# A chunked RWKV-7 recurrence with its state and right-hand sides stored compactly: one head per partition half

## The chip, the cores and the metric

The kernel runs on one core of a Trainium2 chip. The metric is the device time of one execution in microseconds, the median of several runs. A second source is one profiled execution with a record of every instruction; its own time stands beside the median below. TensorE (PE) multiplies, VectorE (DVE), ScalarE (ACT) and GpSimd (POOL) do the elementwise work, SyncE (SP) issues most DMAs.

## The reference

One decoder layer for 256 tokens and a model width of 2048: a normalised input goes through one projection, whose columns feed an RWKV-7 mixer (16 heads of 64) and a latent attention (8 heads); both results are joined, projected and added; a gated feed-forward part with a short convolution follows. The change touches the RWKV-7 recurrence alone:

```python
def step(state, inp):
    r_t, w_t, k_t, v_t, a_t, b_t = inp
    sa = jnp.einsum('bhvk,bhk->bhv', state, a_t)
    state = (state * w_t[:, :, None, :]
             + sa[..., None] * b_t[:, :, None, :]
             + v_t[..., None] * k_t[:, :, None, :])
    return state, jnp.einsum('bhvk,bhk->bhv', state, r_t)

y = rwkv7_scan(r, decay, k, v, -kk, kk * a)
```

Here `kk` is a key divided by its norm, `kk * lax.rsqrt(jnp.maximum(jnp.sum(kk * kk), 1e-24))`. The state of a head is 64 by 64.

## The kernel before

Everything is fp32. Weights come in tiles of 128x1024; for each, SP loads `raw` (L132), ACT rounds it to `hi` (L138), DVE makes `lo = raw - hi` (L139), and PE multiplies `hi` and `lo` with activations (L168 to L202). This stream of weight tiles runs through the whole kernel: the 35 tiles of the input projection (`in_tile`), the tiles of the attention's up-projections (`up_b`), the output projection and the feed-forward part. The order of instructions on each engine is not written out by hand: a planner with a cost model of its own orders them, and each engine then runs its list strictly in order. So instructions of the recurrence stand between weight products on PE, and between casts on ACT and subtractions on DVE.

The recurrence is computed in four chunks of 64 tokens (`chunk(c)`), and in each chunk for two halves of the heads (`hf`), eight heads each. A half has four pairs `a_` of two heads `h`; head 0 of a pair lies on partitions 0 to 63, head 1 on 64 to 127. All products of a chunk come from line 700, with 64 output columns, head 0 to output partitions 0 to 63 and head 1 to 64 to 127, alternating between the heads.

- `px`, the right-hand side: the state times the keys (`state(0)`, from chunk 1 on), plus a local product of 128 rows (`local(0)`).
- `XB` (L711): the right-hand side, taken from `px` by DVE and multiplied there with `mtok`, the reciprocal squared key norms. XB has 128 rows and 128 columns for each pair, and the heads lie on its diagonal blocks; the other blocks were cleared once (L680). Two DVE instructions of 64 partitions each.
- `pu`: the inverse `TT` (128 rows) times XB. It is copied to `UV` by DVE for head 0 and by ACT for head 1 (L717).
- `pS`: the update of the state, 128 rows (keys and values of the chunk).
- `py`: the output, again a state product (`state(1)`) and a local one; ACT copies it to `yt` (L736).
- `ST`, the state: also block diagonal, 128 by 128 for each pair, cleared once (L675). DVE adds `pS` and multiplies with the decay `PC`, for each head by itself: four instructions of 64 partitions (L730, L731), two in chunk 0 (L733).

The inverse of a chunk's 64x64 unit triangular matrix is made ahead of the chunks. Its two 32x32 diagonal blocks are inverted by 31 steps of DVE (`solve`, L589 to L602); there the rows and columns of `Lp` are multiplied with `Mp`, the same norms in another layout (L596), and the diagonal of `Tq` starts at 1 (L594, POOL). The results go to `TT` and `T11` by DMA. The off-diagonal 32x32 corner then takes two sets of 64 small products. In the first (`pR`, L651) the heads alternate; DVE copies the result to `RT` and multiplies it with `mtok` (L655). The second (`pT`, L664) does 16 products of head 0, then 16 of head 1, and DVE copies it to `TT` (L668). Head 0 uses array rows 32 to 63 and columns 0 to 31 there, head 1 rows 96 to 127 and columns 64 to 95.

Behind the recurrence a group normalisation follows for each half of the tokens (L748), mostly on DVE, and then the output projection.

Of the kernel before, what the change touches and what calls it, by code (L numbers as in the profile page):

```python
# [9 lines left out]
F32 = mybir.dt.float32  # L10
# [4 lines left out]
ALU = mybir.AluOpType  # L15
AX = mybir.AxisListType

P = 128
# [36 lines left out]
def hybrid_layer(ctx: ExitStack, tc: tile.TileContext, a: dict, out: bass.AP):  # L55
    nc = tc.nc
    V, S, PE = nc.vector, nc.scalar, nc.tensor
    PSUM = bass.MemoryType.PSUM

    sb = ctx.enter_context(tc.tile_pool(name="sb", bufs=1))  # L60
# [5 lines left out]
    def nm(s):  # L66
        uid[0] += 1
        return f"{s}{uid[0]}"
# [3 lines left out]
    def s4(dt=F32, n="s4"):  # L72
        return sb.tile([P, 1024], dt, tag="s4", name=nm(n), bufs=NS4)

    def sv(n):
        return sb.tile([P, 1024], F32, tag="sv", name=nm(n), bufs=3)
# [13 lines left out]
    def t1(n, w=T, dt=F32):  # L90
        return sb.tile([P, 260], dt, tag="t1", name=nm(n), bufs=NT1)[:, :w]
# [10 lines left out]
    def ch(n="ch"):  # L102
        return ps.tile([P, 512], F32, tag="ch", name=nm(n), bufs=NCH)
# [4 lines left out]
    def con(shape, n, dt=F32):  # L108
        return sb.tile(shape, dt, name=n, bufs=1)
# [299 lines left out]
    AR = [s4(n="AR").rearrange("p (g c s t) -> p g c s t", g=2, c=4, s=2) for _ in range(4)]  # L409
    BK = [s4(n="BK").rearrange("p (g c s t) -> p g c s t", g=2, c=4, s=2) for _ in range(4)]  # L410
    PC = con([P, 8, 4], "PC")
# [46 lines left out]
    for h in range(2):  # L458
        hs = slice(h * 64, h * 64 + 64)
# [29 lines left out]
    mtok = con([P, 32], "mtok")  # L489
    Mp = con([P, 32], "Mp")  # L490
# [89 lines left out]
    TT = con([P, 32, 64], "TT")  # L580
# [8 lines left out]
    def solve():  # L589
        Lp = Lps[0]  # L590
        Tq = sv("Tq").rearrange("p (s t) -> p s t", s=32)
        tm = t1("tm")
        nc.gpsimd.memset(Tq, 0.0)
        nc.gpsimd.memset(Tq.rearrange("p s t -> p (s t)")[:, 0:1024:33], 1.0)  # L594
        nc.gpsimd.memset(TT, 0.0)
        V.tensor_tensor(Lp, Lp, Mp.unsqueeze(1).broadcast_to([P, 32, 32]), ALU.mult)  # L596
        for i in range(31):
            n, m = i + 1, 31 - i
            tv = tm[:, 0:n * m].rearrange("p (s t) -> p s t", s=n)
            V.tensor_tensor(tv, Tq[:, 0:n, i:i + 1].broadcast_to([P, n, m]),  # L600
                            Lp[:, i:i + 1, i + 1:32].broadcast_to([P, n, m]), ALU.mult)
            V.tensor_tensor(Tq[:, 0:n, i + 1:32], Tq[:, 0:n, i + 1:32], tv, ALU.add)  # L602
        dT = dr.tile([P, 32, 32], F32, name="dT")
        nc.sync.dma_start(dT, Tq)
        tp = sv("tp").rearrange("p (s t) -> p s t", s=32)
        V.tensor_copy(tp, Tq.rearrange("p s t -> p t s"))
        dU = dr.tile([2, 32, 32, 32], F32, name="dU")
        for h in range(2):
            T11.append(sv("T11").rearrange("p (q s) -> p q s", q=32))
        for h in range(2):  # L610
            nc.sync.dma_start(dU[h], tp[h * 64:h * 64 + 32])
        for h in range(2):
            nc.sync.dma_start(T11[h][64:96], dU[h].rearrange("q s t -> s q t"))
        for h in range(2):
            for b in range(2):
                k0 = h * 64 + b * 32
                nc.sync.dma_start(TT[k0:k0 + 32, :, b * 32:(b + 1) * 32], dT[k0:k0 + 32].rearrange("q s t -> s q t"))

    pend.append((0, solve_load))
    pend.append((1, solve))  # L620


# [21 lines left out]
    RT = sv("RT").rearrange("p (q s) -> p q s", q=32)  # L644
    for qh in range(2):
        pr_ = ch("pR")
        for q in range(16):
            qq = qh * 16 + q
            for h in range(2):
                o0 = h * 64 + 32  # L650
                PE.matmul(pr_[o0:o0 + 32, q * 32:(q + 1) * 32], G1[qq // 8][qq % 8 // 4][64:96, h * 4 + qq % 4, 32:64],  # L651
                          T11[h][64:96, qq, :], start=True, stop=True, tile_position=(64, o0))
        for h in range(2):
            o0 = h * 64 + 32
            V.tensor_tensor(RT[o0:o0 + 32, qh * 16:(qh + 1) * 16, :],  # L655
                            pr_[o0:o0 + 32].rearrange("p (q s) -> p q s", q=16),
                            mtok[o0:o0 + 32, qh * 16:(qh + 1) * 16].unsqueeze(2).broadcast_to([32, 16, 32]), ALU.mult)
    for qh in range(2):
        pr_ = ch("pT")
        for h in range(2):  # L660
            r0, o0 = h * 64 + 32, h * 64
            for q in range(16):
                qq = qh * 16 + q
                PE.matmul(pr_[o0:o0 + 32, q * 32:(q + 1) * 32], RT[r0:r0 + 32, qq, :],  # L664
                          TT[r0:r0 + 32, qq, 32:64], start=True, stop=True, tile_position=(r0, o0))
        for h in range(2):
            o0 = h * 64
            V.tensor_copy(TT[o0:o0 + 32, qh * 16:(qh + 1) * 16, 32:64],  # L668
                          pr_[o0:o0 + 32].rearrange("p (q s) -> p q s", q=16))


    yt = [sv("yt") for _ in range(2)]
    ST = [con([P, 4, P], f"ST{hf}") for hf in range(2)]
    for hf in range(2):
        nc.gpsimd.memset(ST[hf], 0.0)  # L675


    XB = [sb.tile([P, 512], F32, tag="xs", name=nm("XB"), bufs=2).rearrange("p (a t) -> p a t", a=4) for _ in range(2)]
    for hf in range(2):
        nc.gpsimd.memset(XB[hf], 0.0)  # L680
    HS = (slice(0, 64), slice(64, 128))

    ylast = [None] * 4
# [3 lines left out]
    def chunk(c):  # L687
        w, r = c // 2, c % 2
        rs_ = HS[r]
        for hf in range(2):  # L690
            px = ch("px")
            py = ch("py")

            def pairs(dst, terms):
                for n, term in enumerate(terms):
                    for a_ in range(4):
                        p = hf * 4 + a_
                        for h in range(2):
                            lhsT, rhs = term(p, a_, h)
                            PE.matmul(dst[HS[h], a_ * 64:(a_ + 1) * 64], lhsT, rhs,  # L700
                                      start=n == 0 and a_ == 0, stop=True, skip_group_check=True)

            def state(s):
                return lambda p, a_, h: (AR[p // 2][:, p % 2, c, s, :], ST[hf][:, a_, HS[h]])

            def local(s):
                return lambda p, a_, h: (G1[c][hf][:, h * 4 + a_, s * 64:s * 64 + 64], UV[c][:, p, HS[h]])

            pairs(px, ([state(0)] if c > 0 else []) + [local(0)])
            for h in range(2):  # L710
                V.tensor_tensor(XB[hf][HS[h], :, HS[h]], px[HS[h], 0:256].rearrange("p (a v) -> p a v", a=4),  # L711
                                mtok[HS[h], c * 8 + hf * 4:c * 8 + hf * 4 + 4].unsqueeze(2).broadcast_to([64, 4, 64]),
                                ALU.mult)
            pu = px[:, 256:512]
            pairs(pu, [lambda p, a_, h: (TT[:, c * 8 + p, :], XB[hf][:, a_, HS[h]])])
            for h in range(2):
                (S.copy if h else V.tensor_copy)(UV[c][64:128, hf * 4:hf * 4 + 4, HS[h]],  # L717
                                                 pu[HS[h]].rearrange("p (a v) -> p a v", a=4))
            if c < 3:
                pS = ch("pS")  # L720
                pairs(pS, [lambda p, a_, h: (BKt[c][:, p, HS[h]], UV[c][:, p, HS[h]])])
            pairs(py, ([state(1)] if c > 0 else []) + [local(1)])
            if c < 3:
                for h in range(2):
                    hs = HS[h]
                    sv = ST[hf][hs, :, hs]
                    pSv = pS[hs, 0:256].rearrange("p (a v) -> p a v", a=4)
                    pcb = PC[hs, hf * 4:hf * 4 + 4, c:c + 1].broadcast_to([64, 4, 64])
                    if c > 0:
                        V.tensor_tensor(sv, pSv, sv, ALU.add)  # L730
                        V.tensor_tensor(sv, sv, pcb, ALU.mult)  # L731
                    else:
                        V.tensor_tensor(sv, pSv, pcb, ALU.mult)  # L733
            for h in range(2):
                yv = yt[w][rs_, hf * 512:(hf + 1) * 512].rearrange("p (a h v) -> p a h v", a=4, h=2)
                ylast[c] = S.copy(yv[:, :, h, :], py[HS[h], 0:256].rearrange("p (a v) -> p a v", a=4)).ins  # L736
# [44 lines left out]
    for c in range(4):  # L781
        chunk(c)
# [199 lines left out]
    for blk, nf in enumerate((24, 20)):  # L982
        hh = [s4(F32R, "hh").rearrange("p (k t) -> p k t", k=4) for _ in range(nf // 4)]
        hl = [s4(F32R, "hl").rearrange("p (k t) -> p k t", k=4) for _ in range(nf // 4)]
        for fi in range(nf):
            f = f0 + fi
# [28 lines left out]
        for c in range(4):  # L1015
            accs = [mm() for _ in range(2)]
            for i in range(n - (4 if blk == 1 and c == 3 else 0)):
                prod_a(accs, piece(a["wdn"][c, f0 // 2 + i]), h_hi, h_lo, i * 2, 2, i == 0, i == n - 1)
                if blk == 1 and i == 2:
                    q = n - 4 + c  # L1020
# [98 lines left out]
```

## Time and profile before

| | us |
|---|---|
| median of 3 runs | 1200.92 (1199.66 to 1203.73) |
| profiled execution | 1200.7 |
| its span, first to last instruction | 1198.9 |

The page of the profile gives the busy time of each engine; PE's busy time is that of its matmuls and PEld's that of the loads of the stationary operand, which overlap them. The view by stage gives the same for chosen stretches of the span, with the granted TensorE clock (1.00 is full speed) and the share of the DMA engines. The chain that ended last lists, in order of time, the work that set the end: each piece is what released the next. The groups give, for each line and shape, the number of instructions, their busy time and mean, the idle time of the engine just before them, and what ended it. An fp32 matmul appears as two records.

In this profile the corner products run from about 233 to 244 us, and the four chunks from 244 to 316 us.

### The profile page before, as it was taken

Reading aid. Unit: us, or ns where it says so; the run is one execution under the profiler, and the core shown is the slowest. Engines: PE = TensorE matmul, PEld = TensorE weight load, DVE = VectorE, ACT = ScalarE, POOL = GpSimd, SP = SyncE. Lnnn points to the kernel's source line nnn. Section 1 sums busy time; section 2 is a strip of 40 time slices with the busy share of each in tenths; the row PEclk is TensorE's granted clock in tenths of the full one; section 3 lists DMA queues with packets and bytes.
Section 4 is the critical chain, followed back from the end, with each engine's and each line's share of the span. In section 5 each row is a group of like instructions: output and inputs, shape, how many; then the busy total and the mean of one; then the engine's idle time right before and its main releaser. Section 6 shows DMA issues by size and latency. Waiting matters only on the chain.

```text
span 1198.9 us, 19411 instructions
## 1 busy us (share of the span) xinstructions
PE 1168.8 (97%) x7673; PEld 1028.4 (86%) x7673; DVE 822.0 (69%) x1326; ACT 586.7 (49%) x887; POOL 33.2 (3%) x92
## 2 busy tenths in 40 slices
PE   9999999997989999999999999999999999999996
PEld 8899999996877888888888888888888888888885
DVE  5988669866986566777777775444577777775653
ACT  6694345432434455655555554333455555554541
POOL 1200000101000001000000000000000000000000
PEclk9999999989999999999999999999999999999999
DMA  9635455724333555655555565565655555566662
GB/s 315 217 106 177 133 171 191 229 90 128 107 106 123 178 179 171 206 187 191 192 190 194 189 197 180 193 196 188 209 188 188 191 191 191 194 226 204 209 210 82
DMA packets 71036, 215.99 MB, mean 180 GB/s; under 512 B 17616, under 2 KB 17872, under 8 KB 70944
## 3 DMA queue, kind: packets, MB, share of 16 engines
q1 hardware_dynamic: 69776, 211.84, 54.4%
q10 hardware_dynamic: 768, 2.05, 0.5%
q8 instruction: 60, 0.98, 0.4%
q0 software_dynamic: 400, 0.85, 0.3%
q14 instruction: 32, 0.26, 0.1%
HBM read 210.58 MB, written 3.41 MB: 178 GB/s over the span
## 4 chain that ended last, share of the span: by engine, by line
PE 91%; DVE 4%; DMA 2%; ACT 1%; POOL 1%; issue 1%; SPq 0%; ACTq 0%; DVEq 0%; POOLq 0%
PE mm L168 27%; PE mm L171 14%; PE mm L178 11%; PE mm L200 9%; PE mm L201 9%; PE mm L202 9%; PE mm L181 5%; DMA raw<-in_win 2%; PE pg L545 1%; DMA xt<-in_x 1%; DVE lo L139 1%; PE px L700 1%; ACT hi L138 0%; PE pT L664 0%; PE py L700 0%
## 5 line engine op out<-in xcount | busy, mean ns | idle before, releaser
L139 DVE TENSOR_TENSOR lo<-raw,hi 128x1024 fp32r<-128x1024 f32 x376 | 460.0, 1224 | 285.8 <-ACT hi L138 280.0
L138 ACT CAST hi<-raw 128x1024 fp32r<-128x1024 f32 x376 | 395.1, 1051 | 477.7 <-issue 146.8
L168 PE MATMUL mm<-z,hi 128*128 128x512 f32 x1408 | 351.2, 392 | 0.0
L168 PEld LDWEIGHTS mm<-z,hi 128*128 128x128 f32 x1408 | 251.9, 188 | 43.7
L171 PEld LDWEIGHTS mm<-z,lo 128*128 128x128 f32 x1408 | 188.2, 188 | 14.5
L171 PE MATMUL mm<-z,lo 128*128 128x256 f32 x1408 | 191.5, 278 | 0.0
L178 PE MATMUL mm<-x,hi 128*128 128x256 f32 x1024 | 138.8, 285 | 1.9 <-ACT hi L138 1.9
L178 PEld LDWEIGHTS mm<-x,hi 128*128 128x128 f32 x1024 | 126.8, 191 | 5.4 <-ACT hi L138 2.3
L201 PE MATMUL mm<-lo,hh 128*128 128x512 f32 x336 | 130.7, 389 | 0.0
L202 PE MATMUL mm<-hi,hl 128*128 128x512 f32 x336 | 130.7, 389 | 0.0
L200 PE MATMUL mm<-hi,hh 128*128 128x512 f32 x336 | 119.7, 389 | 0.0
L202 PEld LDWEIGHTS mm<-hi,hl 128*128 128x128 f32 x336 | 63.1, 188 | 13.2
L200 PEld LDWEIGHTS mm<-hi,hh 128*128 128x128 f32 x336 | 63.1, 188 | 13.0
L201 PEld LDWEIGHTS mm<-lo,hh 128*128 128x128 f32 x336 | 63.0, 188 | 13.0
L181 PE MATMUL mm<-x,lo 128*128 128x256 f32 x512 | 74.1, 283 | 0.0
L181 PEld LDWEIGHTS mm<-x,lo 128*128 128x128 f32 x512 | 65.7, 191 | 0.9 <-issue 0.7
L201 PE MATMUL mm<-lo,yhi 128*128 128x512 f32 x128 | 51.6, 403 | 0.0
L202 PE MATMUL mm<-hi,ylo 128*128 128x512 f32 x128 | 50.1, 393 | 0.0
L200 PE MATMUL mm<-hi,yhi 128*128 128x512 f32 x128 | 49.2, 402 | 0.0
L200 PEld LDWEIGHTS mm<-hi,yhi 128*128 128x128 f32 x128 | 23.9, 188 | 5.6 <-issue 0.8
L201 PEld LDWEIGHTS mm<-lo,yhi 128*128 128x128 f32 x128 | 24.1, 188 | 4.9 <-DVE lo L139 0.3
L202 PEld LDWEIGHTS mm<-hi,ylo 128*128 128x128 f32 x128 | 24.1, 188 | 4.9
(280 smaller groups left out, 1078.7 us busy)
## 6 DMA issues: line engine op xcount, KB each, us to landing
raw<-in_wgu SPq DMA_DIRECT2D x176, 512.0 KB, 3.4
raw<-in_wdn SPq DMA_DIRECT2D x88, 512.0 KB, 4.1
raw<-in_win SPq DMA_DIRECT2D x70, 512.0 KB, 3.8
raw<-in_wout SPq DMA_DIRECT2D x32, 512.0 KB, 3.5
raw<-in_wuq SPq DMA_DIRECT2D x6, 512.0 KB, 3.4
xraw<-in_xT SPq DMA_DIRECT2D x4, 512.0 KB, 6.8
xt<-in_x SPq DMA_DIRECT2D x4, 512.0 KB, 7.4
raw<-in_wuv SPq DMA_DIRECT2D x4, 512.0 KB, 3.3
```

Of the source, the lines that this page charges most:

```text
L138: S.copy(hi, raw)
L139: last_lo[0] = V.tensor_tensor(lo, raw, hi.bitcast(F32), ALU.subtract).ins
L168: PE.matmul(acc, hi[:, j * P:(j + 1) * P], act(kt0 + j), start=first and j == 0, stop=False, skip_group_check=True)
L171: PE.matmul(acc[:, :T], lo[:, j * P:(j + 1) * P], act(kt0 + j)[:, 0, :], start=False, stop=last and j == n - 1, skip_group_check=True)
L178: PE.matmul(acc[:, :T], hi[:, j * P:(j + 1) * P], act(kt0 + j)[:, s, :], start=first and j == 0 and s == 0, stop=False)
L181: PE.matmul(acc[:, :T], lo[:, j * P:(j + 1) * P], act(kt0 + j)[:, 0, :], start=False, stop=last and j == n - 1)
L200: PE.matmul(accs[tb], ah, wh, start=first and j == 0, stop=False)
L201: PE.matmul(accs[tb], ah, wl, start=False, stop=False)
L202: PE.matmul(accs[tb], al, wh, start=False, stop=last and j == n - 1)
L545: PE.matmul(pg[h][:, o:o + P], BK[pp][hs, gg, w * 2 + r, :, :], AR[pp][hs, gg, w * 2 + r, :, :], start=o == 0, stop=True, skip_group_check ...
L700: PE.matmul(dst[HS[h], a_ * 64:(a_ + 1) * 64], lhsT, rhs, start=n == 0 and a_ == 0, stop=True, skip_group_check=True)
```

## The change

State and right-hand side are no longer block diagonal. `ST` and `XB` hold 256 columns for a half: four pairs of 64, with head 0 on partitions 0 to 63 and head 1 on 64 to 127. The state products and the products with `TT` then take 64 rows for each head, instead of 128 rows of which half met zeros. The clearing of ST and XB is dropped. The updates of ST become one instruction for both heads.

The norms `mtok` are no longer multiplied onto XB and RT. The diagonal of `Tq` starts at `Mp` instead of 1, so that the inverse comes out with the norms in it. XB and RT are then plain copies: XB by DVE for half 0 and by ACT for half 1; RT and the corner of TT by DVE for head 0 and by ACT for head 1. In the second set of corner products the heads alternate.

```diff
-        nc.gpsimd.memset(Tq.rearrange("p s t -> p (s t)")[:, 0:1024:33], 1.0)
+        V.tensor_copy(Tq.rearrange("p s t -> p (s t)")[:, 0:1024:33], Mp)
...
-            V.tensor_tensor(RT[o0:o0 + 32, qh * 16:(qh + 1) * 16, :],
-                            pr_[o0:o0 + 32].rearrange("p (q s) -> p q s", q=16),
-                            mtok[o0:o0 + 32, qh * 16:(qh + 1) * 16].unsqueeze(2).broadcast_to([32, 16, 32]), ALU.mult)
+            (S.copy if h else V.tensor_copy)(RT[o0:o0 + 32, qh * 16:(qh + 1) * 16, :],
+                                             pr_[o0:o0 + 32].rearrange("p (q s) -> p q s", q=16))
...
-        for h in range(2):
-            r0, o0 = h * 64 + 32, h * 64
-            for q in range(16):
-                qq = qh * 16 + q
+        for q in range(16):
+            qq = qh * 16 + q
+            for h in range(2):
+                r0, o0 = h * 64 + 32, h * 64
                 PE.matmul(pr_[o0:o0 + 32, q * 32:(q + 1) * 32], RT[r0:r0 + 32, qq, :],
                           TT[r0:r0 + 32, qq, 32:64], start=True, stop=True, tile_position=(r0, o0))
         for h in range(2):
             o0 = h * 64
-            V.tensor_copy(TT[o0:o0 + 32, qh * 16:(qh + 1) * 16, 32:64],
-                          pr_[o0:o0 + 32].rearrange("p (q s) -> p q s", q=16))
+            (S.copy if h else V.tensor_copy)(TT[o0:o0 + 32, qh * 16:(qh + 1) * 16, 32:64],
+                                             pr_[o0:o0 + 32].rearrange("p (q s) -> p q s", q=16))
...
-    ST = [con([P, 4, P], f"ST{hf}") for hf in range(2)]
-    for hf in range(2):
-        nc.gpsimd.memset(ST[hf], 0.0)
+    ST = [con([P, 256], f"ST{hf}") for hf in range(2)]
...
-                return lambda p, a_, h: (AR[p // 2][:, p % 2, c, s, :], ST[hf][:, a_, HS[h]])
+                return lambda p, a_, h: (AR[p // 2][HS[h], p % 2, c, s, :], ST[hf][HS[h], a_ * 64:(a_ + 1) * 64])
...
-            for h in range(2):
-                V.tensor_tensor(XB[hf][HS[h], :, HS[h]], px[HS[h], 0:256].rearrange("p (a v) -> p a v", a=4),
-                                mtok[HS[h], c * 8 + hf * 4:c * 8 + hf * 4 + 4].unsqueeze(2).broadcast_to([64, 4, 64]),
-                                ALU.mult)
+            (S.copy if hf else V.tensor_copy)(XB[hf], px[:, 0:256])
             pu = px[:, 256:512]
-            pairs(pu, [lambda p, a_, h: (TT[:, c * 8 + p, :], XB[hf][:, a_, HS[h]])])
+            pairs(pu, [lambda p, a_, h: (TT[HS[h], c * 8 + p, :],
+                                         XB[hf][HS[h], a_ * 64:(a_ + 1) * 64])])
...
-                    if c > 0:
-                        V.tensor_tensor(sv, pSv, sv, ALU.add)
-                        V.tensor_tensor(sv, sv, pcb, ALU.mult)
-                    else:
-                        V.tensor_tensor(sv, pSv, pcb, ALU.mult)
+                if c > 0:
+                    V.tensor_tensor(ST[hf], pS[:, 0:256], ST[hf], ALU.add)
+                    V.tensor_tensor(s4v, s4v, pcb, ALU.mult)
+                else:
+                    V.tensor_tensor(s4v, pS[:, 0:256].rearrange("p (a v) -> p a v", a=4), pcb, ALU.mult)
```

Here `s4v` is ST of the half seen as four pairs of 64 columns.

More of the change, by code (lines that the diff above doesn't have):

```diff
@@ L667, in hybrid_layer @@
             o0 = h * 64
-            V.tensor_copy(TT[o0:o0 + 32, qh * 16:(qh + 1) * 16, 32:64],
-                          pr_[o0:o0 + 32].rearrange("p (q s) -> p q s", q=16))
+            (S.copy if h else V.tensor_copy)(TT[o0:o0 + 32, qh * 16:(qh + 1) * 16, 32:64],
+                                             pr_[o0:o0 + 32].rearrange("p (q s) -> p q s", q=16))
     yt = [sv("yt") for _ in range(2)]
-    ST = [con([P, 4, P], f"ST{hf}") for hf in range(2)]
-    for hf in range(2):
-        nc.gpsimd.memset(ST[hf], 0.0)
-    XB = [sb.tile([P, 512], F32, tag="xs", name=nm("XB"), bufs=2).rearrange("p (a t) -> p a t", a=4) for _ in range(2)]
-    for hf in range(2):
-        nc.gpsimd.memset(XB[hf], 0.0)
+    ST = [con([P, 256], f"ST{hf}") for hf in range(2)]
+    XB = [sb.tile([P, 512], F32, tag="xs", name=nm("XB"), bufs=2)[:, 0:256] for _ in range(2)]
     HS = (slice(0, 64), slice(64, 128))
@@ L723, in chunk @@
             if c < 3:
[L724 to L728, printed above, removed]
-                    if c > 0:
-                        V.tensor_tensor(sv, pSv, sv, ALU.add)
-                        V.tensor_tensor(sv, sv, pcb, ALU.mult)
-                    else:
-                        V.tensor_tensor(sv, pSv, pcb, ALU.mult)
+                pcb = PC[:, hf * 4:hf * 4 + 4, c:c + 1].broadcast_to([P, 4, 64])
+                s4v = ST[hf].rearrange("p (a v) -> p a v", a=4)
+                if c > 0:
[3 more added lines that the diff above has]
+                    V.tensor_tensor(s4v, pS[:, 0:256].rearrange("p (a v) -> p a v", a=4), pcb, ALU.mult)
             for h in range(2):
```

## The prediction

> **What bounds the kernel now.** I read the first two parts of the page, then the busy time by stage, then the chain that ended last inside the recurrence, and last the groups of instructions in that stretch.
>
> ```profile
> span 1198.9 us, 19411 instructions
> PE 1168.8 (97%) x7673; PEld 1028.4 (86%) x7673; DVE 822.0 (69%) x1326; ACT 586.7 (49%) x887; POOL 33.2 (3%) x92
> ```
>
> By the page PE is the bound: 97% of the span. That share is an average. The stages (columns: stretch, its length, busy time of PE, PEld, DVE, ACT, POOL, then the granted clock, the DMA share, GB/s) show where it is not true:
>
> ```profile
> 225.00:238.00 13.00, 13.00 (x220) 12.65 (x219) 8.12 (x13) 4.11 (x5) 4.49 (x14) 1.00 0.95 267
> 238.00:241.40 3.40, 2.79 (x82) 2.55 (x80) 2.92 (x6) 0.52 (x1) 0.00 (x0) 1.00 0.50 163
> 241.40:248.00 6.60, 6.56 (x80) 6.38 (x81) 2.67 (x5) 0.00 (x0) 0.00 (x0) 0.51 0.19 74
> 248.00:276.00 28.00, 28.00 (x306) 25.21 (x306) 18.28 (x32) 12.79 (x21) 1.77 (x5) 0.99 0.36 114
> 276.00:312.00 36.00, 25.79 (x520) 22.13 (x519) 27.25 (x59) 10.24 (x21) 3.94 (x14) 0.95 0.29 93
> 312.00:341.00 29.00, 29.00 (x217) 25.53 (x217) 22.66 (x39) 11.34 (x18) 0.00 (x0) 1.00 0.45 146
> 341.00:369.00 28.00, 22.90 (x97) 15.94 (x96) 20.81 (x53) 7.52 (x21) 0.00 (x0) 0.88 0.18 57
> 369.00:1199.00 830.00, 820.09 (x4329) 704.08 (x4327) 540.09 (x754) 408.28 (x596) 4.57 (x14) 1.00 0.58 189
> ```
>
> Three things stand out. After 369 us PE is full, and the change touches nothing there. At 241.4 to 248 PE is busy but at clock 0.51: about 3.2 of the 6.6 us are lost. At 276 to 312, where most of the recurrence runs, PE is idle for 10.2 of 36 us and DVE is busy for 27.25. So a microsecond counts in full before 276, where PE is the bound, and it counts in 276 to 312 if it lies on the chain of waits. What is gained there stays gained, since the weight products behind are in order on PE.
>
> The chain at the start of the recurrence (start, duration, work):
>
> ```profile
> 229.59 1.81 PE mm L178 x16
> ...
> 234.01 2.14 PE pR L651 x124
> ...
> 238.41 2.38 PE pT L664 x78
> 240.79 0.65 issue
> 241.44 2.60 PE pT L664 x50
> 244.04 1.05 PE px L700 x16
> 245.09 3.48 PE mm L178 x15
> ...
> 258.51 0.61 PE px L700 x16
> ...
> 292.03 0.47 PE py L700 x16
> ```
>
> and what DVE does in one round of it (a round is one half of the heads in one chunk; start, duration, instructions):
>
> ```profile
> 286.28 0.88 DVE L730 TENSOR_TENSOR ST<-pS,ST 64x256 f32<-64x256 f32 x2 [2.18 <-PE pS L700]
> 287.19 0.87 DVE L731 TENSOR_TENSOR ST<-ST,PC 64x256 f32<-64x256 f32 x2
> 288.09 0.69 DVE L757 TENSOR_REDUCE gmu<-yt 128x8 f32<-128x512 f32 x1
> 288.81 0.86 DVE L711 TENSOR_TENSOR XB<-px,mtok 64x256 f32<-64x256 f32 x2
> ```
>
> In this round the state takes four DVE instructions in a row and the row block XB two, and PE stands behind them. That is the serial part that the change shortens.
>
> **The change part by part.**
>
> *Corner products.* An fp32 product shows as two records. The pR products alternate between the heads' output columns and start every 2.14/124 = 17.3 ns. The pT products take all of one head, then the other, and start every 2.38/78 = 30.5 ns in the part before the clock falls. With the heads alternating I price all 128 at pR's spacing: 2.21 us. Now they take 2.38 + 2.60 = 4.98 us and a gap of 0.65 us, whose cause the profile doesn't show, so I leave it in. Saved 2.77. Then the clock: the pR run, of the same 32-row form and 2.14 us long, kept 1.00 (first row of stages); the fall comes after the longer pT run and its gap. With a run of 2.2 us I take it that the clock stays. Then px takes 0.61 and not 1.05 (saved 0.44), and 15 L178 products take 15/16 x 1.81 = 1.70 and not 3.48 (saved 1.78). Together 5.0 us, in a stretch where PE is the bound. Ends: 5.6 if the gap goes too; 1.9 if the clock falls as before (78 x 17.3 ns, 50 at twice that, and the gap make 3.7 against 5.6); 0 if alternating brings nothing, which is a rival.
>
> *XB and ST on 128 partitions.* The groups of 276 to 312 us:
>
> ```profile
> L711 DVE TENSOR_TENSOR XB<-px,mtok 64x256 f32<-64x256 f32 x10 | 4.2, 421 | 0.2
> L730 DVE TENSOR_TENSOR ST<-pS,ST 64x256 f32<-64x256 f32 x8 | 3.4, 420 | 3.7 <-PE pS L700 3.5
> L731 DVE TENSOR_TENSOR ST<-ST,PC 64x256 f32<-64x256 f32 x8 | 3.3, 418 | 0.2
> ...
> L190 DVE TENSOR_TENSOR qn<-mm,rrB 128x256 f32<-128x256 f32 x1 | 0.4, 425 | 0.0
> ```
> ```profile
> L717 ACT COPY UV<-px 64x256 f32<-64x256 f32 x4 | 1.5, 367 | 18.5 <-DVE UV L717 18.5
> ```
>
> An instruction of 256 columns takes 0.42 us on 64 partitions and on 128 (the L190 row), so two become one at the price of one. Of 10 XB instructions here, 4 belong to half 0 and become 2; 6 belong to half 1 and become 3 copies on ACT at 0.37 us. The 16 ST instructions become 8. DVE loses 8 x 0.421 + 4 x 0.420 + 4 x 0.418 = 6.7 us of its 27.25. On the chain one round gets shorter by half of each pair above: 0.44 + 0.43 + 0.43 = 1.3 us. There are four such rounds in the stretch (XB came ten times there, that is five pairs, and the last of them has no state behind it), so I take 4 x 1.3 = 5.2 us. The ends are 0, if something else holds the round (a rival), and the whole 6.7.
>
> What ACT takes over, and the wait ahead of the inverse (mean ns of one, then the idle time before):
>
> ```profile
> L138 ACT CAST hi<-raw 128x1024 fp32r<-128x1024 f32 x376 | 395.1, 1051 | 477.7 <-issue 146.8
> L655 DVE TENSOR_TENSOR RT<-pR,mtok 32x512 f32<-32x512 f32 x4 | 2.8, 690 | 1.4 <-PE pR L651 1.3
> L668 DVE COPY TT<-pT 32x512 f32<-32x512 f32 x4 | 2.7, 684 | 2.6 <-PE pT L664 2.6
> L596 DVE TENSOR_TENSOR Lp<-Lp,Mp 128x1024 f32<-128x1024 f32 x1 | 1.2, 1227 | 1.4 <-DMA Lp<-dL 1.4
> ```
>
> ACT gets four XB copies in the recurrence. It is busy 10.24 of 36 us in this stretch; what is queued behind a waiting copy there are the copies of U and y of the same half, which need its result anyway, and at times a weight cast, for which PE would wait. An XB copy stuck behind such a cast costs up to one cast, 1.05 us by the L138 row, times three.
>
> *RT and TT copies.* Two of each pair go from DVE to ACT, which runs them side by side. Cover: while RT is made (235.2 to 238.0), PE works on L178 and L181 products, so nothing is gained there; without that cover it would be 1.4 us (two instructions of 0.69 us, L655). TT's last copy ends before px's rows are needed.
>
> *Norms in the inverse.* The diagonal of Tq becomes one DVE copy of 32 elements instead of a GpSimd memset. It needs Mp and the cleared Tq, both long there, and DVE waits 1.4 us for Lp just before L596 (last row): cost nothing; uncovered, less than the 0.42 us of 256 columns. The dropped memsets of ST and XB were on an engine with 3% busy: nothing.
>
> *64-row products.* State and XB products, 192 + 128 = 320 records, go from 128 rows by 64 columns to 64 by 64. Heads already lie in different column halves, so two already run side by side; 16 records take 0.47 us (py at 292.03), 29 ns each. I take the same spacing after. Bounds: pR's 17.3 ns as a floor (320 x 12 ns = 3.8 us gain), and a loss that is the first rival.
>
> *Changes of row form on PE.* This is new. Now all products of a chunk have one form. After the change state products (64 rows) stand between local and pS products (128 rows). The weight loads show what a change of form costs:
>
> ```profile
> 232.91 0.20 PEld L651 LDWEIGHTS pR<-T,G 32*32 32x32 f32 x4
> 233.15 0.65 PEld L178 LDWEIGHTS mm<-x,hi 128*128 128x128 f32 x5
> 233.94 0.65 PEld L651 LDWEIGHTS pR<-T,G 32*32 32x32 f32 x36
> ```
>
> Four pR loads at 17 ns would let the next start at 232.98; it starts at 233.15. Five L178 loads at 1.81/16 = 113 ns would end at 233.72; pR starts at 233.94. So 0.2 us for each change, for 32x32 against the full array. [...]
>
> A round has four changes that no wait covers: pS to y-state and back, y-local to the next x-state, x-state to x-local. Two lie between the copy of U and the state update; the others run while DVE works on ST. So 2 x 0.2 x 4 rounds = 1.6 us on the chain, and 4 x 0.2 = 0.8 us for the round before 276, where PE is full: cost 2.4 us. Ends: 0, and all four changes in all six rounds with a state, 4.8.
>
> *Sum.* Profiled execution: 1200.7 us (span 1198.9 and 1.8 around it). 1200.7 - 5.0 - 5.2 + 2.4 = 1192.9. The median of the runs, 1200.92, lies 0.2 higher, so 1193.1.
>
> **The rivals.**
>
> *Slower: the two heads' 64-row products exclude each other.* Both heads write the same PSUM tile (px, py, one bank) from different row halves, as do the alternating pT products. In the kernel before, 64-row products of two heads (pg, L545) write two tiles. If two row halves can't write one bank at once, they run one after the other: the step from 17.3 to 30.5 ns between pR and pT is a factor 1.77, and 16 records go from 0.47 to 0.83 us. There are 12 state and 8 XB batches: 20 x 0.36 = 7.2 us, all taken as on the path. The corner products gain nothing and the clock falls as before. 1200.7 - 5.2 + 2.4 + 7.2 = 1205.1. The point from which it decides is (5.2 - 2.4)/20 = 0.14 us per batch. [...] Chance 0.13.
>
> *The round doesn't shrink.* DVE's freed time is refilled: gmu (at 288.09) already sits between ST and XB, and in 276 to 312 DVE has other normalisation work that goes into any gap; ACT's casts may hold XB. Then only the corner gains: 1200.7 - 5.0 + 2.4 = 1198.1. Chance 0.13.
>
> *The corner isn't freed.* Alternating gives no speed, or the clock falls all the same because the run of small products follows pR more closely: 1200.7 - 5.2 + 2.4 = 1197.9 at worst, 1196.0 with 1.9 kept. Chance 0.14.
>
> **How the numbers follow.** The forecast, 1193.1, has 0.60, and its own range is 1187 to 1197 (corner 5.6, DVE 6.7 and no cost of form give 1188.6, a third of the 3.8 for faster 64-row products 1187; 4.8 for form and a corner of 3.5, near the middle of its two ends with a gain, give 1197). The range reaches to the two rivals around 1198, and to 1201 for one of these with the dearer changes of form, and leaves out the slower one: 1187 to 1201. A measurement of this kernel can tell about 0.3%, 3.6 us, from no change; the borders are 1197.3 and 1204.5. Faster: 0.60 and half of the corner rival's 0.14, and a little of the other, 0.69. Slower: the first rival, 0.13; what part of it ends inside the border is made up by a tail in which the other two meet the dearer changes of form. The same: the rest, 0.18.
>
> **What would show it.** Right: the pT group in about 2.2 us with starts near 17 ns and a clock near 1.00 at 241 to 248; XB and ST as 128x256 instructions near 0.42 us, half as many; idle PE in the recurrence well under 10 us; gaps near 0.2 us where a state product follows a local one. Wrong: 64-row batches of 16 over 0.7 us; pT still at 30 ns; rounds between two copies of U as long as before with something new in the place of the second ST and XB; a new stop on ACT before XB; or a difference after 369 us, where this working expects none.

## The result and the profile after

| kernel | median, us | lowest to highest | runs |
|---|---|---|---|
| before | 1199.68 | 1196.34 to 1203.73 | 9 |
| after | 1193.76 | 1191.29 to 1195.77 | 9 |

The ratio after to before is 0.9949, 95% interval 0.9934 to 0.9963, a gain of 6.1 ± 1.7 us at 1200. The forecast was 1193.1 us. The profiled execution of the kernel after took 1195.8 us.

The page of the kernel after, its head and the busy time by engine:

```profile
span 1193.9 us, 19389 instructions
...
PE 1168.3 (98%) x7673; PEld 1027.1 (86%) x7673; DVE 809.4 (68%) x1301; ACT 590.0 (49%) x895; POOL 31.9 (3%) x87
```

PE has as many products as before. DVE has 25 instructions fewer. The span is 5.0 us shorter. Where it was saved is told by the first product of the feed-forward part (line 168). The view of that line shows the first and the last start, first in the kernel before:

```profile
L168 PE MATMUL mm<-z,hi x1408: 387/392/481, 462.8 to 1078.8; 128*128 128x512 f32 x176
```

and in the kernel after:

```profile
L168 PE MATMUL mm<-z,hi x1408: 387/392/481, 457.8 to 1073.8; 128*128 128x512 f32 x176
```

The first start is 5.0 us earlier and so is the last. All of the gain lies ahead of 458 us. It can be split at the corner. From the first pT record to the record behind the seventh L181 record that follows, both profiles do the same work on PE (128 records of pT, 16 of px, 15 of L178, 7 of L181). That took 10.87 us before and takes 9.95 after, which is 0.9 us. From there to the first L168 it was 213.6 us and is 209.3, which is 4.3 us. PE is busy for 198.3 and 198.5 us of that, so what shrank there is its idle time. (The pT products start 0.2 us later.) The stages of the kernel after, in the columns of the prediction:

```profile
238.00:241.40 3.40, 2.69 (x84) 2.29 (x82) 1.81 (x2) 1.08 (x2) 0.00 (x0) 1.00 0.59 233
241.40:248.00 6.60, 6.12 (x86) 5.94 (x87) 1.10 (x2) 1.85 (x3) 0.00 (x0) 0.55 0.25 83
...
276.00:312.00 36.00, 29.23 (x528) 24.66 (x524) 27.02 (x53) 13.09 (x27) 1.89 (x4) 1.00 0.33 105
...
341.00:369.00 28.00, 24.00 (x107) 17.20 (x106) 22.97 (x58) 9.98 (x28) 0.00 (x0) 0.94 0.24 78
```

In the recurrence (276 to 312) PE's idle time fell from 10.2 to 6.8 us. DVE's busy time there hardly moved (27.25 to 27.02): what it lost was filled with the next work of its list. The clock in this stretch is 1.00 and was 0.95, which the prediction did not count on. Against the forecast stands the second row: the clock is 0.55 behind the corner, where the prediction took 1.00. The chain that ended last shows the corner of this execution:

```profile
239.44 1.26 PE pT L663 x72
240.69 1.18 issue
241.88 1.62 PE pT L663 x54
243.50 1.05 PE px L695 x16
244.55 2.65 PE mm L178 x11
```

Each row is start, duration and work; "issue" is time in which PE waited for nothing that the profile shows. The pT products now start every 1.26/72 = 17.5 ns, as forecast. But the stop in their midst grew from 0.65 to 1.18 us, and the products behind it run at the lower clock: px takes 1.05 us, as before.

The rounds of the recurrence, from the same chain of the kernel after (px is the product with XB where it follows XB):

```profile
280.21 0.64 PE px L695 x16
...
284.93 0.33 DVE XB L705
...
290.52 0.38 ACT XB L705
...
292.19 1.23 DVE qr L829
293.42 1.15 DVE qs L830
294.59 1.22 DVE qr L831
295.81 0.35 DVE ST L720
296.18 0.43 DVE ST L721
...
298.22 0.34 DVE XB L705
```

and of the kernel before:

```profile
282.52 1.15 PE px L700 x16
...
289.24 0.44 DVE XB L711
...
295.22 0.44 DVE XB L711
...
302.54 0.43 DVE XB L711
```

XB was complete at 289.68, 295.66 and 302.97 before, and is at 285.26, 290.90 and 298.56 after. Taken from the first px, the rounds lasted 7.2, 6.0 and 7.3 us before and last 5.1, 5.6 and 7.7 us after. Two rounds shrank, by 2.1 and 0.4 us. Of the 2.1 us, most hangs on the point from which the round is counted: XB was ready 1.8 us ahead of that px after the change, while PE worked on other products, so from XB to XB this round shrank by 0.4 us only. The third grew by 0.4: three instructions of the attention's normalisation (qr, qs, qr) now stand ahead of ST there, where the chain before had the ST pair between qs and the second qr.

The groups of 276 to 312 us in the kernel after:

```profile
L721 DVE TENSOR_TENSOR ST<-ST,PC 128x256 f32<-128x256 f32 x4 | 1.7, 425 | 0.1
L720 DVE TENSOR_TENSOR ST<-pS,ST 128x256 f32<-128x256 f32 x4 | 1.7, 420 | 3.3 <-PE pS L695 3.3
L705 ACT COPY XB<-px 128x256 f32<-128x256 f32 x3 | 1.1, 373 | 1.0 <-PE px L695 1.0
L705 DVE COPY XB<-px 128x256 f32<-128x256 f32 x2 | 0.8, 416 | 0.0
```

An instruction of 256 columns on 128 partitions costs what one on 64 did (0.42 us on DVE, 0.37 on ACT). ACT begins these three XB copies when px is there; no weight cast held them.

### The profile page after: what moved, and what is told of

Its sections match the earlier page's. It is cut to its first block, busy times and chain, and to the rows that moved or that the text cites. A ratio compares the mean times of both kernels' runs of the same rounds, so it can differ in the third digit from the quotient of the medians.

```text
span 1193.9 us, 19389 instructions
## 1 busy us (share of the span) xinstructions
PE 1168.3 (98%) x7673; PEld 1027.1 (86%) x7673; DVE 809.4 (68%) x1301; ACT 590.0 (49%) x895; POOL 31.9 (3%) x87
## 4 chain that ended last, share of the span: by engine, by line
PE 92%; DVE 4%; DMA 2%; ACT 1%; issue 1%; POOL 0%; SPq 0%; ACTq 0%; DVEq 0%
PE mm L168 27%; PE mm L171 14%; PE mm L178 11%; PE mm L200 9%; PE mm L201 9%; PE mm L202 9%; PE mm L181 5%; PE pg L545 1%; PE px L695 1%; DMA xraw<-in_xT 1%; DMA xt<-in_x 1%; DVE lo L139 1%; PE py L695 1%; DMA raw<-in_win 0%; PE lw L426 0%
## 5 line engine op out<-in xcount | busy, mean ns | idle before, releaser
L168 PE MATMUL mm<-z,hi 128*128 128x512 f32 x1408 | 351.2, 392 | 0.0
L168 PEld LDWEIGHTS mm<-z,hi 128*128 128x128 f32 x1408 | 251.9, 188 | 43.7
L178 PE MATMUL mm<-x,hi 128*128 128x256 f32 x1024 | 139.0, 284 | 1.3 <-ACT x L148 1.2
L178 PEld LDWEIGHTS mm<-x,hi 128*128 128x128 f32 x1024 | 126.7, 191 | 5.0 <-issue 1.7
L181 PE MATMUL mm<-x,lo 128*128 128x256 f32 x512 | 75.1, 285 | 0.0
L181 PEld LDWEIGHTS mm<-x,lo 128*128 128x128 f32 x512 | 66.6, 193 | 1.0 <-issue 0.7
```

The source lines that it names most:

```text
L168: PE.matmul(acc, hi[:, j * P:(j + 1) * P], act(kt0 + j), start=first and j == 0, stop=False, skip_group_check=True)
L178: PE.matmul(acc[:, :T], hi[:, j * P:(j + 1) * P], act(kt0 + j)[:, s, :], start=first and j == 0 and s == 0, stop=False)
L181: PE.matmul(acc[:, :T], lo[:, j * P:(j + 1) * P], act(kt0 + j)[:, 0, :], start=False, stop=last and j == n - 1)
```

## The experiments

The prediction is the main theory; its view of the corner, half of the gain or more, is called B. Two rival theories stand beside it. A: all of the gain comes from the merged XB and ST (one instruction for both heads), and the corner is worth less than 1 us. C: the gain comes from 64-row products. The other letters are explained where they come up. Each ratio is to the kernel before, measured in the same group of runs. A difference of two ratios is given in us (times 1200), with the two half-widths added in squares. The planner orders the instructions of each kernel anew, so a difference between two kernels holds the new order as well.

| kernel | median, us (runs) | ratio, 95% interval |
|---|---|---|
| first group: before | 1199.32 (35) | |
| only the corner order changed (corner_alone) | 1197.56 (12) | 0.9982 [0.9967, 0.9997] |
| after, corner order as before (no_corner) | 1196.68 (12) | 0.9976 [0.9963, 0.9989] |
| after, XB and ST one instruction for each head (split_heads) | 1200.74 (12) | 1.0015 [0.9998, 1.0032] |
| the same with 128-row products (rows128) | 1198.10 (12) | 0.9989 [0.9975, 1.0003] |
| second group: before | 1199.84 (23) | |
| after again (after_again) | 1193.46 (8) | 0.9948 [0.9930, 0.9967] |
| after, more warm-up products (shift64) | 1204.07 (10) | 1.0043 [1.0023, 1.0062] |
| before with compact, merged XB and ST (merge_alone) | 1197.18 (12) | 0.9986 [0.9970, 1.0002] |
| after, py's local products first (order_py) | 1192.31 (6) | 0.9938 [0.9913, 0.9963] |
| third group: before | 1200.37 (14) | |
| after, py's local products first (order_again) | 1193.62 (9) | 0.9949 [0.9928, 0.9969] |
| after a third time (after_third) | 1194.19 (6) | 0.9949 [0.9930, 0.9968] |
| before, one execution (before_look) | 1198.10 (1) | |
| no_corner, one execution (no_corner_look) | 1195.94 (1) | |

**The corner alone, and everything but the corner.** The first kernel is the one before with the two loops of the pT products exchanged:

```diff
-        for h in range(2):
-            r0, o0 = h * 64 + 32, h * 64
-            for q in range(16):
-                qq = qh * 16 + q
+        for q in range(16):
+            qq = qh * 16 + q
+            for h in range(2):
+                r0, o0 = h * 64 + 32, h * 64
                 PE.matmul(pr_[o0:o0 + 32, q * 32:(q + 1) * 32], RT[r0:r0 + 32, qq, :],
```

The second is the kernel after with the opposite edit.

> The kernel before with one edit: the second set of corner products (pT) alternates between the heads. Theory A (the whole gain of the change comes from XB and ST being one instruction for both heads; the corner gives under 1 us, because PE stops inside the run for something that is not a product, and the clock falls in any case): pT records start every 17 ns instead of 30, the stop inside the run grows from 0.65 to about 1.2 us, the clock still falls to half for about 6.8 us, time within 1 us of before (1199.7). Theory B (the corner carries half or more of the gain): 1195 to 1197, with a shorter stretch at half clock.

> The changed kernel with the second set of corner products undone (16 of one head, then 16 of the other). Theory A: at most 1 us slower than the changed kernel, 1194 to 1195. Theory B: it loses half of the gain or more, 1196.5 to 1199.

Measured: the corner alone saves 2.2 ± 1.8 us (ratio 0.9982). Taken out of the kernel after, it costs 0.9976 - 0.9949 = 0.0027, that is 3.2 ± 2.4 us. A's bound of 1 us lies inside both intervals, and so does B's half (3 us), so the medians alone decide little: they put the corner at some 2 to 3 us, not 5. The profiles say more. The stretch of equal work described above took 9.8 to 10.9 us in the five profiles with the old order (mean 10.5). With the new order it took 6.2 to 6.9 us in the six profiles in which the clock stayed at 1.00 behind the corner (mean 6.5), and 9.3 to 10.0 us in the three in which it fell (mean 9.6). So the order is worth 4.0 us where the clock stays, 0.8 us where it falls, and 2.9 us on the average of the nine. That speaks against A and puts the corner near B's half. A had also expected the clock to fall in corner_alone, where it stayed at 1.00 (with a stop of 0.94 us). The chain of no_corner shows what the order costs when the clock falls:

```profile
236.93 2.38 PE pT L663 x78
239.31 0.27 issue
239.57 1.97 PE pT L663 x50
241.54 1.05 PE px L695 x16
242.60 3.50 PE mm L178 x15
```

These are the 30.5 ns of the kernel before (2.38/78), and the same 1.05 and 3.5 us behind them.

**The merged instructions and the row form.** The third kernel keeps everything of the kernel after but gives each head its own XB and ST instruction on 64 partitions (`HS[h]` and `hs` are the rows of a head):

```diff
-            (S.copy if hf else V.tensor_copy)(XB[hf], px[:, 0:256])
+            for h in range(2):
+                (S.copy if hf else V.tensor_copy)(XB[hf][HS[h]], px[HS[h], 0:256])
...
-                    V.tensor_tensor(ST[hf], pS[:, 0:256], ST[hf], ALU.add)
-                    V.tensor_tensor(s4v, s4v, pcb, ALU.mult)
+                        V.tensor_tensor(ST[hf][hs], pS[hs, 0:256], ST[hf][hs], ALU.add)
+                        V.tensor_tensor(s4v, s4v, pcb, ALU.mult)
```

The fourth makes ST and XB block diagonal again on top of that, so that all products of a chunk have 128 rows; the norms in the inverse, the ACT copies and the corner order are what is left of the change:

```diff
-                return lambda p, a_, h: (AR[p // 2][HS[h], p % 2, c, s, :], ST[hf][HS[h], a_ * 64:(a_ + 1) * 64])
+                return lambda p, a_, h: (AR[p // 2][:, p % 2, c, s, :], ST[hf][:, a_, HS[h]])
...
-            pairs(pu, [lambda p, a_, h: (TT[HS[h], c * 8 + p, :],
-                                         XB[hf][HS[h], a_ * 64:(a_ + 1) * 64])])
+            pairs(pu, [lambda p, a_, h: (TT[:, c * 8 + p, :], XB[hf][:, a_, HS[h]])])
```

> The changed kernel with XB and ST made by one instruction for each head again (64 partitions each, same engines, same 64-row products). Theory A: each of four rounds gets 1.3 us longer, PE idle in the recurrence goes back from 6.8 towards 10 us, 1198 to 1200. Theory C (the gain is that of the 64-row products on PE): 1194, no slower than the changed kernel.

> As split_heads, but state and XB block diagonal again, with 128-row products: only the norms in the inverse, plain copies and the corner are left of the change. Theory A: no changes of row form on PE, so it is 1 to 2.5 us faster than split_heads (0.16 us for each change of form, two to four in a round, six rounds), 1196 to 1198. Theory C: slower than split_heads, 1199 to 1201.

Measured: without merging the kernel is 1.0015 - 0.9949 = 0.0066 slower than the kernel after, 7.9 ± 2.7 us, and slower than the kernel before or equal to it. 64-row products in place of 128-row ones cost 1.0015 - 0.9989 = 0.0026, 3.1 ± 2.6 us; they save nothing, which speaks against C, as does the time without merging (C forecast 1194). What is left in rows128 beyond the corner (norms, ACT copies) is 0.9989 - 0.9982 = 0.0007, 0.8 ± 2.5 us, no difference that this can tell from nothing. So by these differences the merging is the whole net gain beside the corner, and the compact layout that makes it possible costs some of it.

How merging saves its time is only in part what the prediction says. The stage of the recurrence in split_heads:

```profile
276.00:312.00 36.00, 27.40 (x445) 23.70 (x445) 27.89 (x55) 12.81 (x26) 0.00 (x0) 0.89 0.22 70
```

The granted clock in this stretch is 0.86 to 0.95 in the five profiles with XB and ST by head (0.95 before and in corner_alone, 0.86, 0.91 and 0.89 in before_look, rows128 and split_heads). In the nine with merged instructions it is 1.00 six times and 0.95 three times. By the means, 0.91 and 0.98, that is up to 0.07 x 36 = 2.5 us, an estimate from above, since PE is idle in part of the stretch. What keeps the clock up there was not tested.

**The price of a change of row form.** The weight loads of PE in one round of the kernel after (start, duration; the form is in the middle):

```profile
288.50 0.55 PEld L695 LDWEIGHTS py<-UV,G 128*64 128x64 f32 x14
289.12 0.54 PEld L695 LDWEIGHTS px<-ST,AR 64*64 64x64 f32 x16
289.74 0.55 PEld L695 LDWEIGHTS px<-UV,G 128*64 128x64 f32 x16
```

and in the kernel before, where both have 128 rows:

```profile
277.74 0.60 PEld L700 LDWEIGHTS px<-ST,AR 128*64 128x64 f32 x16
278.21 0.60 PEld L700 LDWEIGHTS px<-UV,G 128*64 128x64 f32 x16
```

From the first state load to the first local load it is 0.62 us now and was 0.47: 0.15 us for the change, against 0.2 for the other pair of forms in the prediction. K is the theory that each change costs its 0.16 us in full, L that the changes are hidden in PE's idle time. An edit takes two of the four changes of a round away: the local products of py ahead of its state products, so that the next px state products follow their own form:

```diff
-            pairs(py, ([state(1)] if c > 0 else []) + [local(1)])
+            pairs(py, [local(1)] + ([state(1)] if c > 0 else []))
```

> The changed kernel with the two terms of py exchanged: local products first, then state products, so that on PE the state products of py and of the next px stand together and a round has two uncovered changes of row form instead of four. Theory K (a change of form costs 0.16 us of PE, on the chain or where PE is full): six rounds x 2 x 0.16 = 1.9 us less, 1191.5 to 1193. Theory L (they are hidden in PE's idle time, and state products as filler while U is copied are worth more): the same as the changed kernel or up to 2 us slower.

> The kernel after with the local products of py ahead of its state products, so that the next right-hand side's state products follow products of their own form: two changes of form fewer in each round. Theory K (a change of form costs 0.16 us where PE is the last to arrive: two fewer in four rounds on the chain and in the round before): 1.3 to 1.6 us less than the kernel after in the same call. Theory L (hidden behind DVE's state update): no difference, within 0.5 us. The first run of this edit stood 1.2 us below, with overlapping intervals.

In its loads the two changes are gone (order_again):

```profile
286.52 0.54 PEld L695 LDWEIGHTS py<-ST,AR 64*64 64x64 f32 x16
286.98 0.55 PEld L695 LDWEIGHTS px<-ST,AR 64*64 64x64 f32 x16
287.60 0.55 PEld L695 LDWEIGHTS px<-UV,G 128*64 128x64 f32 x16
```

State follows state after 0.46 us. In 276 to 312 us PE's idle time is 36.00 - 31.11 = 4.9 us, against 6.8 in the third execution of the kernel after. First order_again, then after_third:

```profile
276.00:312.00 36.00, 31.11 (x489) 27.39 (x488) 27.52 (x52) 13.81 (x26) 0.00 (x0) 1.00 0.37 117
```

```profile
276.00:312.00 36.00, 29.23 (x501) 24.87 (x502) 26.93 (x52) 13.26 (x28) 0.46 (x1) 1.00 0.32 103
```

These windows do not hold the same work, though: the last copy of y ends at 317.2 us in order_again and at 311.4 in after_third, so other weight products stand in between. By the medians the edit saves 1.2 us in the second group and 0.6 in the third; the intervals overlap in both, and in the third the two ratios are equal (0.9949). The loads show that the changes are gone; whether that saves time is not settled between L's 0 and K's 1.6 us.

**Everything but the norms, the ACT copies and the corner.** The kernel before with compact ST and XB, one DVE instruction for both heads, and the norms still multiplied onto XB:

```diff
-            for h in range(2):
-                V.tensor_tensor(XB[hf][HS[h], :, HS[h]], px[HS[h], 0:256].rearrange("p (a v) -> p a v", a=4),
-                                mtok[HS[h], c * 8 + hf * 4:c * 8 + hf * 4 + 4].unsqueeze(2).broadcast_to([64, 4, 64]),
-                                ALU.mult)
+            V.tensor_tensor(XB[hf].rearrange("p (a v) -> p a v", a=4), px[:, 0:256].rearrange("p (a v) -> p a v", a=4),
+                            mtok[:, c * 8 + hf * 4:c * 8 + hf * 4 + 4].unsqueeze(2).broadcast_to([P, 4, 64]), ALU.mult)
```

and ST and its products as in the kernel after. J is the theory that XB's move to ACT counts, too.

> The kernel before with compact ST and XB only: 64-row products, one instruction for both heads, XB always by VectorE and still multiplied with the norms there; the norms in the inverse, the copies on ScalarE and the alternating corner are left out. Theory A (the merged instructions carry the gain, the norms and ScalarE nothing): as fast as the changed kernel without the corner, 1195.5 to 1197.5. Theory J (taking XB of half 1 off VectorE counts too): 1198 to 1199.5.

Measured: 1.7 ± 1.9 us faster by the ratio, 2.7 by the medians. The prediction's terms for this edit are -5.2 + 2.4 = -2.8 us. That is not told apart from no change by itself, but agrees in size, and the median of 1197.18 lies where A expected it (1195.5 to 1197.5), not J (1198 to 1199.5). By the ratios J is not settled: what this kernel lacks against the kernel after (corner, norms, ACT copies) is 0.9986 - 0.9949 = 0.0037, 4.4 ± 2.6 us, of which the corner's 2 to 3 us leave about 2, inside the error.

**The stop and the clock in the corner.** The kernel after was run twice more. The expectations weigh two theories on the fall of the clock: F, it belongs to the order of the products, against G, it is chance. (So the letters stand from after_third on; in after_again G stands for the kernel's order.) They also weigh H, PE's stop is a block of its instructions that comes late, against I, it belongs to the products.

> The changed kernel once more, beside the next ones. All theories: 1193 to 1195. [...] Theory G (the fall belongs to this kernel's order): the same fall as in the first profile.

> The kernel after once more, as the comparison for the new order and as a third look at the corner. Theory F (the fall of the clock behind the corner belongs to the head-by-head order and to a long stop): 1.00 in the stretch behind the corner. Theory G (it is chance in either order): 1.00 or 0.5, as in the first two looks.

> The kernel before, one look, for the clock behind the corner. Theory F: it falls to about 0.5 again for some 7 us, as in the three profiles with the head-by-head order so far. Theory G: 1.00 in about half of the looks; then the medians hold only half of the 2.2 us that the first profile shows behind the corner.

> The kernel after with the second set of corner products head by head again, a second look, for the clock. Theory F: falls to about 0.5. Theory G: 1.00 in about half of the looks.

The corner of after_again, from the chain and from the stages:

```profile
240.29 1.26 PE pT L663 x72
241.55 0.36 issue
241.91 1.07 PE pT L663 x54
242.97 0.61 PE px L695 x16
243.59 1.47 PE mm L178 x11
```

```profile
241.40:248.00 6.60, 6.24 (x128) 5.83 (x122) 3.42 (x6) 2.22 (x4) 0.00 (x0) 1.00 0.28 86
```

The same kernel, with a stop of 0.36 us instead of 1.18, kept the clock at 1.00; this is the picture of the forecast. In after_third it fell again, to 0.51. Over all profiles the counts are:

| pT order | profiles | clock fell behind the corner | stop where it fell, us | stop where it stayed, us |
|---|---|---|---|---|
| head by head | 5 | 5 | 0.65, 0.27, 0.29, 0.38, 0.83 | |
| alternating | 9 | 3 | 1.18, 0.91, 0.63 | 0.94, 0.91, 0.36, 0.27, 0.20, and shift64 without a stop within pT |

Neither holds as stated. With the heads one behind the other the clock fell in every execution seen (its mean over 241.4 to 248 us was 0.51 to 0.74), as F says; with the heads alternating it fell in three of nine (0.51 to 0.58), never with a stop under 0.6 us, and with 0.91 us both ways. Of the kernel after itself, it fell in two of three. So the order matters and chance has a part, and a threshold isn't to be read from this.

The stop comes after 78 records of pT in the kernel before, and after 2 + 4 + 72 = 78 records counted from the same point in the kernel after (four of them from L178). In all thirteen profiles but that of shift64 it comes ahead of the same record of PE's list, number 2132 counted from 0. To move it without touching the products, 52 instead of 20 warm-up products were put at the start of the kernel, 64 records more:

```diff
-    for _ in range(20):
+    for _ in range(52):
```

> The changed kernel with 52 instead of 20 warm-up products at the start of PE's program, that is 64 more records and nothing else in the code. Theory H (PE's stop inside pT is the next block of its instructions arriving late; in all six kernels so far it comes after the same number of PE instructions): the stop moves 64 records earlier, to about record 10 to 14 of pT, and a further one may come 128 records later, about 10 records into px. Theory I (the stop belongs to the products, to their data or to the second result tile): it stays after record 74 of pT. Time 1192 to 1197 by H, 1193 to 1195 by I.

```profile
247.85 2.14 PE pT L663 x126
249.98 0.43 PE px L695 x9
250.42 0.75 issue
251.17 0.45 PE px L695 x7
```

The pT products now run through, at 2.14/126 = 17.0 ns each, and the stop stands in the midst of px. That refutes I: the stop doesn't belong to the pT products. Nor does it stay at one place in PE's list. At record 2132, which is now the 15th from the start of pT and where H expected the stop first, PE runs on; the stop comes ahead of record 2259, 127 further on, where H expected a later one. So the possible places lie about 128 records apart, and whether PE stops at one differs. In the kernel after, the page has these packets for the whole span,

```profile
q8 instruction: 60, 0.98, 0.4%
```

and the view by DMA queue for 236 to 242 us has one of them:

```profile
q8 instruction: 1, 0.02, 1.1%
```

PE has 7673 records of products and as many of weight loads, and 7673/60 = 128 products for each packet, close to the 127 between the two places; no other engine on the page has more than 1301 instructions. Behind 480 us, too, the trace has 29 of these packets for 3755 products, 129 for each. That the queue carries PE's instructions is the author's inference from these counts. Taken so, places about 128 records apart fit H; that PE waits there for a packet is not shown. The time of shift64, 1204.07 us where 1192 to 1197 was expected, is no measure of the corner: its warm-up records take until 15.5 us, those of the kernel after until 8.4, and everything behind starts later.

## Why the prediction was right

The sum came out: 1193.1 forecast, 1193.76 measured. Part of that closeness is luck. The forecast was a gain of 7.8 us, counted from a median of 1200.92 for the kernel before. With nine runs that median is 1199.68, and the gain is 5.9 us by the medians and 6.1 by the ratio. So the gain is 1.7 to 1.9 us smaller than forecast, and the lower starting point hides most of that. The corner gave too little; the merging net of the changes of form, 2.8 us by the forecast, gave as much or more (2.9 us in no_corner, 4.2 us in the profiles). The terms, in the order of the prediction:

- **Corner, -5.0 forecast: mis-sized.** Measured 3.2 ± 2.4 and 2.2 ± 1.8 us by the medians, 2.9 us by the profiles. The spacing of 17.3 ns was right (17.5 and 17.0 measured). What failed is the step "with a run of 2.2 us I take it that the clock stays". It stayed in six of nine profiles with this order, and fell in the one that came with the result. Where it stayed the order gave 4.0 us, where it fell 0.8, not the 1.9 of the prediction's lower end. That the gap would stay as it is also failed: it does not belong to the pT products (in shift64 they run through, and PE stops in px for 0.75 us), and it ran from 0.20 to 1.18 us in the other thirteen profiles.
- **XB and ST merged, -5.2 forecast:** 7.9 ± 2.7 us by split_heads, and 1.7 + 3.1 = 4.8 ± 3.2 us by merge_alone and the price of the form. The term is at the edge of the first interval and inside the second. Its own picture, four rounds each shorter by 1.3 us, was not exact: in the profile two rounds shrank by 2.1 and 0.4, and one grew by 0.4 where other DVE work came ahead of ST. From the end of the corner to line 168 the three profiles of the kernel after (209.0 to 210.1 us) are 4.2 us shorter on average than those of before, before_look and corner_alone (213.6 to 213.8). By the estimate above, up to 2.5 us of the merging can come by way of the clock in the recurrence, for which the prediction has no term.
- **Changes of row form, +2.4 forecast:** 3.1 ± 2.6 us measured by split_heads against rows128, which differ in the products themselves and in their order, too. The 0.2 us for each was read from 32x32 products beside 128x128 ones; that a change between 64x64 and 128x64 costs as much was the author's estimate, which no run shows. The loads show 0.15 us in its place. Taking two of the four changes of a round away saved 1.2 and 0.6 us by the medians, which doesn't settle how much of the term is on the path.
- **RT and TT copies, norms, ACT copies, 0 forecast:** 0.8 ± 2.5 us. The fear of a cast ahead of XB on ACT didn't come true: its idle time before XB was 1.0 us in all, ended by px.
- **64-row products, no change forecast:** 16 loads take 0.54 us (0.60 before), and in order_again state follows state after 0.46 us, against 0.47 between two sets of 16 in the kernel before.
- **After 369 us, nothing forecast:** the first and the last start of line 168 moved by the same 5.0 us.

The rivals. *The two heads' products exclude each other:* refuted. The alternating pT products write one tile, at different partitions, from different row quarters, with a start every 17.0 to 17.5 ns, and 16 loads of 64 rows take 0.54 us, where this rival had 0.83. On the order of the corner, the traces show a start every 30.5 ns where pT takes one head after the other, and every 17.0 to 17.5 ns where the heads alternate; pR, whose heads share rows 64 to 95 and differ in columns, starts every 17.3 ns too. *The round doesn't shrink:* false for the whole, since without merging the gain is gone, but true for one round of the three compared. *The corner isn't freed:* half of it is what the profile after happened to show, with the faster spacing and the fallen clock (0.9 us gained in that pair of profiles). Six of nine profiles with the new order do not show it.

## What to carry to other kernels

An elementwise instruction of 256 columns cost the same on 64 and on 128 partitions here (0.42 us on DVE, 0.37 on ACT), so laying two heads on the two partition halves and handling them in one instruction halves such work. That was the larger part of the gain. Smaller products were no faster here (a set of 16 follows the last after 0.46 us with 64 rows, 0.47 with 128), and mixing them with full-height ones cost 0.15 us of PE at a change of form; whether putting products of one form together pays for itself stayed open. Where a term rests on the clock staying up behind a run of tiny products, compare several executions before pricing it in full: here it fell in three of nine. And compare stretches of equal work rather than fixed windows: they told the size of the corner better than the medians.

## What the runs showed of the hardware beyond the forecast

- PE stopped for 0.20 to 1.18 us ahead of record 2132 in thirteen profiles, with nothing in the profile that it waited for. With 64 records put ahead (shift64) it stopped 127 records further on in its list instead, for 0.75 us. The page counts one packet of the instruction queue for 128 products (7673/60); that PE waits for these packets was not shown.
- Behind 128 records of 32x32 products head by head (4.0 to 5.0 us without the stop) the granted clock fell in five of five profiles, to 0.51 to 0.74 as the mean of 241.4 to 248 us; alternating, in three of nine, to 0.51 to 0.58.
- In the recurrence (276 to 312 us) the granted clock was 0.86 to 0.95 where XB and ST took one instruction for each head, and 0.95 to 1.00 where they were merged.
- pT products of two row quarters into one tile, at different partitions, started every 17.0 to 17.5 ns (shift64, after).
- A change between 64x64 and 128x64 products cost 0.15 us on PE: 0.62 us from load to load in the kernel after, 0.47 in the kernel before without a change.
- An instruction of 256 columns took 0.42 us on DVE and 0.37 us on ACT, on 64 and on 128 partitions.
